# A recurrent and linear-attention decoder step: samples' output half a unit later, output sums 10 units behind the heads' opening, two tiles loaded with the others, heads' buffers 96 bytes on

## The chip, the cores and the metric

The kernel runs on one core of one Trainium2 chip. The time is that of the device for one execution, in microseconds, and what counts is the median over the runs of a kernel. The engines of the core each take their instructions in their own order: TensorE (PE in the profile, its weight loads PEld), VectorE (DVE), ScalarE (ACT), GpSimd (POOL) and SyncE (SP). The last two mostly issue transfers here, ScalarE some of them. An instruction that waits holds up all that stand behind it on its engine.

## What is computed

One layer for one prompt of 2048 tokens and for 8 samples of one token each, with a model width of 1024. Cut to what matters:

```
ada = silu(c) @ w_ada + b_ada;  shift, scale, gate = split(ada, 3)
hn  = rmsnorm(x, g_norm) * (1 + scale) + shift
xa, za, q, k, v, glr, zg = split(hn @ w_in)          # one projection, 5136 columns
# group 1: a convolution over 4 tokens, gates, and a linear recurrence over tokens
xc  = conv_b + sum(xp[:, j:j+T] * conv_w[j] for j in range(4))
a   = exp(8 * sigmoid(xc @ w_gate_a + b_a) * log_sigmoid(lambda))
h_t = a_t * h_(t-1) + sqrt(1 - a_t^2) * sigmoid(xc @ w_gate_x + b_x) * xc
y_lru = h * silu(za)
# group 2: 4 heads of gated linear attention (key width 128, value width 256)
S_t = exp(log_alpha_t) * S_(t-1) + k_t^T v_t;   o_t = q_t S_t
y_gla = rmsnorm(o) * g_gla_norm * silu(zg)
y = rmsnorm(x + gate * (concat(y_lru, y_gla) @ w_out), g_final)
```

The outputs are y for the prompt and the samples and the new states of both groups. Everything is float32.

## The kernel before

A float32 product is made of three matmuls on two parts of each operand: a rounded part (names in h: `hh`, `xh`, `vh`) and the rest (names in l: `hl`, `xl`, `vl`). So most matmuls come in threes, such as L661 to L663 for projections and L346 to L348 for the values of a head. For the larger products the kernel uses seven sub-products of half the size instead of eight, with sums of operands prepared ahead.

The prompt is worked off in two halves of 1024 tokens; the samples ride behind the second half. In each half the four heads come in the order 3, 0, 1, 2 (`gla_head`), each followed by tiles of the recurrence (`lru`). Between the halves lie the products of the second half that are made by seven (`sums`, `gates_seven`, `lru_seven`), with buffers of a pool `sp` of their own. Last comes the output product (L1846).

The second half's input comes in eight tiles of 128 tokens, two to a group. `hn_load` (L245) reads the two tiles of a group, on SyncE; `normalize` takes their squares on ScalarE (L165), a reciprocal root on VectorE in twelve small instructions (L147 to L153), and scales the tiles (L181); `modulate` turns them on TensorE (L197) into `hh` and `hl`. `next_hn` (L1428) is called in small pieces between the projections of the last recurrence tile of the first half and of what follows. Tiles 2 to 6 lie in three buffers `xst` of pool `sp`; tiles 0, 1 and 7 lie in a ring `xt`.

A queue of due times sets the order of most of the work in the heads. `after(units, fn)` (L701) puts a step off until the clock has gone on by so many units; `tick` (L705) moves the clock on, about one unit to a projection, and runs what is due. In the second half a head's samples are handled by `sample_state` (L1091), twice, for four samples each: GpSimd issues a load of the head's states (L1100), ScalarE and VectorE update them (L1104, L1105), and three units later `sample_out` (L1109) takes the output on TensorE (L1114), adds both fours (L1119), takes the mean square (L165 and twelve small instructions) and scales the output (L1124). Then it calls `done`, which puts the output in `os_`.

The head's own output is `gla_out` (L1156): TensorE turns the output of the prompt's tokens (L1162), for the last segment puts the samples' output behind them (L1164), and VectorE multiplies both with the gate (L1167). `finish` (L1213) calls it, and for the last segment looks every half unit whether `os_` is there. The fourth head's last steps are run by `flush_gla`, with no projections of a next head between them.

`out_weights` (L800) makes the sums of the output weights ("output sums") in 16 steps. A step loads two blocks of the weights (L829, GpSimd), four units later multiplies them by the gate (two L850 of 128x512), takes four differences (L850, 128x256), in half of the steps splits two of them into two parts (L854 on ScalarE, L855 on VectorE), and stores all (L857, L864, GpSimd) for the output product. It stops ahead of the second half's products and goes on in `close_sp` (L1476), which opens the heads' pools `gp` and `hp` for the second half:

```
        if outw["next"] < 16:
            outw["stop"] = False
            after(4, lambda: out_weights(outw["next"]))
```

On VectorE these sums stand in one order with the work of the heads: the eviction of a chunk's output (L1081), the scaling of a segment's output (L1089), the convolution (L1278) and the split of its result (L1303).

Of the kernel before, what the change touches and what calls it, by code (L numbers as in the profile page):

```python
# [8 lines left out]
F32 = mybir.dt.float32  # L9
# [5 lines left out]
P = 128  # L15
# [34 lines left out]
def dram(ap, off, pattern):  # L50
    return bass.AP(tensor=ap.tensor, offset=ap.offset + off, ap=pattern)
# [3 lines left out]
def hybrid_kernel(ctx, tc, i, o):  # L55
# [127 lines left out]
    def normalize(pool, xt, m=P, tag="f512"):  # L183

        times(xt, scales(pool, squares(pool, xt, m, tag), len(xt), m), m)
# [59 lines left out]
    def hn_load(g, now=True):  # L245

        xt = []
        for j in range(2):
            q = 2 * g + j
            if q in (0, 1, 7):  # L250
                x = xp.tile([P, TH + NS], F32, tag="xt", name="xt")[:, :D]
            else:
                n = q - 2
                x = xst[n // 2][:, n % 2]
            t0 = TH + q * P
            SP.dma_start(x, i["x_prompt"][0, t0:t0 + P])
            xt.append(x)
        if now:
            normalize(xp, xt)
        return xt  # L260
# [176 lines left out]
    with tc.tile_pool(name="ada", bufs=1, side="right") as ap:  # L437
# [79 lines left out]
        with in_order():  # L517
# [24 lines left out]
            for c in range(1, 4):  # L542
                k = (2 * c, 2 * c + 1)
# [100 lines left out]
    gp = gpx.enter_context(tc.tile_pool(name="gp", bufs=1, side="right", reuse_waits="tile"))  # L644
# [56 lines left out]
    def after(units, fn, gla=False, val=False):  # L701
        clock[1] += 1
        heapq.heappush(pend, (clock[0] + units, clock[1], fn, gla, val))
# [10 lines left out]
    def flush_gla():  # L714
        while any(e[3] for e in pend):
            e = min(e for e in pend if e[3])
            pend.remove(e)
            heapq.heapify(pend)
            e[2]()
# [28 lines left out]
    outw = {"stop": False, "next": None, "busy": False}  # L748
# [342 lines left out]
    def sample_state(h, smp, b0, st, done):  # L1091

        if b0 == 0:
            st[:] = [cp.tile([P, NS, 32], F32, tag="sc", name="qm"), gp.tile([P, DV], F32, tag="os", name="os")]
            V.memset(st[0], 0.0)
        qm = st[0]
        vb = xp.tile([P, 4, DV], F32, tag="xt", name="xt")
        G.dma_start(vb, dram(vsd, (h * NS + b0) * DV, [[0, P], [DV, 4], [1, DV]]))
        s0 = xp.tile([P, 4, DV], F32, tag="xt", name="xt")
        G.dma_start(s0, i["state_gla"][0, b0:b0 + 4, h].rearrange("b k v -> k b v"))  # L1100
        for n in range(4):
            b = b0 + n
            V.tensor_copy(qm[:, b, b:b + 1], smp[:, 0, b:b + 1])
            S.activation(s0[:, n], s0[:, n], AF.Copy, scale=smp[:, 2, b:b + 1])  # L1104
            V.scalar_tensor_tensor(s0[:, n], vb[:, n], smp[:, 1, b:b + 1], s0[:, n],  # L1105
                                   op0=OP.mult, op1=OP.add)
        after(3, lambda: sample_out(h, b0, st, s0, done), True)
# [62 lines left out]
    def gla_head(half, h, wv=None, ahead=None):  # L1170
# [13 lines left out]
        prep, zs, os_, state = {}, {}, [None], []  # L1184
# [32 lines left out]
            gla_out(half, h, s, prep[s, "run"][1], os_[0] if s == 2 else None, [zs[s, 0], zs[s, 1]])  # L1217

        def sample(smp, b0):
            sample_state(h, smp, b0, state, lambda: os_.__setitem__(0, state[1]))  # L1220

        pk = None
        if not wv:
# [194 lines left out]
    def lru(half, js, wx=None):  # L1418
        xa_load, xa_unit, za_load, za_unit = lru_units(half)
        for j in js:  # L1420
            t = xa_load(j, wx)
            for s in range(len(t.segs)):
                xa_unit(t, s)
            za_load(t)
            for s in range(len(t.segs)):
                za_unit(t, s)

    def next_hn(xt, g, k):  # L1428

        modulate(xt[g], g, (k, k + 2))  # L1430
        if (g, k) == (0, 6):
            xt.append(hn_load(3, False))
        if (g, k) == (1, 2):
            normalize(xp, xt[3])

    def lru_last_a(js):

        xa_load, xa_unit, za_load, za_unit = lru_units(0)
        xt = [hn_load(0)]
        lru(0, js[:-2])  # L1440
        outw["stop"] = True
        lru(0, js[-2:-1])
        t = xa_load(js[-1])
        za_load(t)
        flush_gla()
        while outw["busy"]:
            heapq.heappop(pend)[2]()
        open_sp()
        xt += [hn_load(1), hn_load(2)]
        for s in range(2):  # L1450
            xa_unit(t, s)
            za_unit(t, s)
            for g in range(2 * s, 2 * s + 2):
                for k in range(0, KT, 2):
                    drips.append(lambda g=g, k=k: next_hn(xt, g, k))
# [20 lines left out]
    def close_sp():  # L1476
        nonlocal gp, hp
        spx.close()
        gp = gpx.enter_context(tc.tile_pool(name="gp", bufs=1, side="right", reuse_waits="tile"))
        hp = hpx.enter_context(tc.tile_pool(name="hp", bufs=1, reuse_waits="tile"))  # L1480
        if outw["next"] < 16:
            outw["stop"] = False
            after(4, lambda: out_weights(outw["next"]))

    def a21():
        return [(hh, hl)[u][:, :4, 512:TH] for u in range(2)]
# [190 lines left out]
    flush_gla()  # L1677
    while outw["busy"]:
        heapq.heappop(pend)[2]()
    gpx.close()  # L1680
    hpx.close()

# [375 lines left out]
    smp = {}  # L2058
# [117 lines left out]
    for n in range(2, 16):  # L2176
        g = n - 1
# [17 lines left out]
    for q in range(8):  # L2195
        g, k = 2 + q // 2, q % 2
# [63 lines left out]
```

## Time and profile before

| | us |
|---|---|
| median of 3 runs | 1456.41 |
| the three runs | 1750.81, 1455.38, 1456.41 |
| the profiled execution | 1454.69 |
| its span (first to last instruction) | 1452.9 |
| TensorE busy in it | 1424.1 |
| VectorE busy in it | 1051.5 |
| ScalarE busy in it | 689.6 |
| GpSimd busy in it | 220.0 |

The profile is one execution. Its times count from the start of the span; an engine is busy while an instruction of its own runs, and what it only issues (a transfer) isn't counted. A row of the timeline gives the start, how long it took, the engine, the line of the kernel, the operation and its tiles, and in brackets how long the engine had been idle before it and what ended that. A view of waits adds these up by the instruction that waited and the one that released it. The second half's heads run from about 708 to 1077 us, and the output product starts at about 1128. The mean granted clock of TensorE was 0.998 of full speed.

### The profile page before, as it was taken

How to read it: one execution, taken by the hardware profiler on the slowest of the kernel's cores; microseconds unless marked ns; L12 is line 12 of the kernel's file. 1: busy time of each engine (PE TensorE's matmuls, PEld its weight loads, DVE VectorE, ACT ScalarE, POOL GpSimd, SP SyncE). 2: the span in 40 equal slices, each digit the busy share in tenths (PEclk: the TensorE clock that was granted, in tenths of full speed). 3: DMA queues.
4: the chain of work that ended last, by engine and by line, in shares of the span. 5: the costliest groups of instructions: out<-in, count | busy, mean ns of one | idle time of the engine just before them, and what ended most of it. 6: DMA issues, size and time to landing. Idle time of an engine off the chain costs nothing. (4 is left out here: it accounts for less than half of the span.)

```text
span 1452.9 us, 23584 instructions
## 1 busy us (share of the span) xinstructions
PE 1424.1 (98%) x8741; PEld 1250.8 (86%) x8741; DVE 1051.5 (72%) x2477; ACT 689.6 (47%) x1251; POOL 220.0 (15%) x364
## 2 busy tenths in 40 slices
PE   7999999999999999999999999999999999999998
PEld 5888989899898988778999999999998887788886
DVE  5757657776676688955468687586788986688886
ACT  4644544662545358524353454535557622144342
POOL 0200111212122113100212322323100000000000
PEclk9999999999999999999999999999999999999999
DMA  9755775764666455667846565656562767694453
GB/s 328 268 185 175 260 262 203 249 236 165 199 209 203 148 179 207 207 221 237 292 158 201 186 217 184 220 186 209 184 226 83 276 221 272 232 362 131 139 171 116
DMA packets 161752, 305.33 MB, mean 210 GB/s; under 512 B 12962, under 2 KB 91458, under 8 KB 159197
## 3 DMA queue, kind: packets, MB, share of 16 engines
q1 hardware_dynamic: 106837, 217.39, 43.6%
q0 software_dynamic: 22752, 70.44, 14.3%
q10 hardware_dynamic: 32048, 16.00, 3.7%
q8 instruction: 69, 1.13, 0.3%
q14 instruction: 46, 0.38, 0.1%
HBM read 188.51 MB, written 115.33 MB: 209 GB/s over the span
## 5 line engine op out<-in xcount | busy, mean ns | idle before, releaser
L661 PE MATMUL acc<-hh,w 128*128 128x512 f32 (+3 forms) x1112 | 386.1, 347 | 0.5 <-DVE xb L999 0.2
L662 PE MATMUL acc<-hl,w 128*128 128x512 f32 (+3 forms) x1112 | 375.6, 338 | 0.2 <-DVE hl L205 0.2
L663 PE MATMUL acc<-hh,w 128*128 128x512 f32 (+3 forms) x1112 | 375.1, 337 | 0.0
L662 PEld LDWEIGHTS acc<-hl,w 128*128 128x128 f32 x1112 | 209.3, 188 | 18.1 <-issue 1.2
L661 PEld LDWEIGHTS acc<-hh,w 128*128 128x128 f32 x1112 | 209.2, 188 | 18.1 <-ACT tx L1318 0.9
L663 PEld LDWEIGHTS acc<-hh,w 128*128 128x128 f32 x1112 | 209.1, 188 | 16.3
L1846 PE MATMUL acc<-w,a 128*128 128x512 f32 (+1 forms) x792 | 184.8, 386 | 0.0
L1846 PEld LDWEIGHTS acc<-w,a 128*128 128x128 f32 x792 | 146.8, 188 | 33.2 <-issue 3.4
L346 PE MATMUL acc<-w,hh 128*128 128x256 f32 (+1 forms) x508 | 144.7, 285 | 0.0
L348 PE MATMUL acc<-w,hl 128*128 128x256 f32 (+1 forms) x508 | 143.5, 282 | 0.2 <-DVE hl L228 0.2
L347 PE MATMUL acc<-w,hh 128*128 128x256 f32 (+1 forms) x508 | 143.4, 282 | 0.0
L1846 PE MATMUL tp<-w,a 128*128 128x512 f32 x564 | 136.0, 391 | 0.0
L1846 PEld LDWEIGHTS tp<-w,a 128*128 128x128 f32 x564 | 105.2, 188 | 26.8 <-issue 5.2
L346 PEld LDWEIGHTS acc<-w,hh 128*128 128x128 f32 x508 | 95.5, 188 | 1.3 <-ACT zs L1128 0.4
L348 PEld LDWEIGHTS acc<-w,hl 128*128 128x128 f32 x508 | 96.2, 189 | 0.4 <-DVE hl L228 0.4
L347 PEld LDWEIGHTS acc<-w,hh 128*128 128x128 f32 x508 | 96.0, 189 | 0.2
L1128 ACT ACTIVATE zs<-acc 128x512 f32<-128x512 f32 (+3 forms) x70 | 34.3, 490 | 107.0 <-PE acc L663 104.0
L1696 ACT CAST a<-s 128x512 fp32r<-128x512 f32 x61 | 36.5, 619 | 96.1 <-issue 36.6
L1278 DVE SCALAR_TENSOR_TENSOR cv<-xa,vecT,cv 128x512 f32<-128x512 f32 (+2 forms) x120 | 76.3, 638 | 7.2 <-ACT cv L1276 6.7
L1129 DVE SCALAR_TENSOR_TENSOR zs<-zs,acc 128x512 f32<-128x512 f32 (+3 forms) x70 | 38.4, 548 | 46.7 <-ACT zs L1128 46.7
L957 ACT CAST vh<-acc 128x256 fp32r<-128x256 f32 x56 | 20.5, 369 | 94.2 <-PE acc L348 81.8
L958 DVE TENSOR_TENSOR vl<-acc,vh 128x256 fp32r<-128x256 f32 x56 | 23.3, 420 | 51.1 <-ACT vh L957 51.1
(403 smaller groups left out, 2746.4 us busy)
## 6 DMA issues: line engine op xcount, KB each, us to landing
parts<-w SPq DMA_DIRECT2D x37, 1024.0 KB
w<-parts SPq DMA_DIRECT2D x28, 1024.0 KB
wr<-in_w_in_dram SPq DMA_DIRECT2D x38, 512.0 KB
a<-mixd SPq DMA_DIRECT2D x63, 256.0 KB
w<-wd SPq DMA_DIRECT2D x12, 1024.0 KB
w<-twd SPq DMA_DIRECT2D x20, 512.0 KB
mixd<-zs ACTq DMA_DIRECT2D x34, 256.0 KB
wada<-in_w_ada_dram SPq DMA_DIRECT2D x16, 512.0 KB
```

What stands on the lines that cost most here:

```text
L346: PE.matmul(ps, hh[:, kt, c], hi[:, kt % 4], start=kt == 0, stop=False)
L347: PE.matmul(ps, hh[:, kt, c], lo[:, kt % 4], start=False, stop=False)
L348: PE.matmul(ps, hl[:, kt, c], hi[:, kt % 4], start=False, stop=kt == KT - 1)
L661: PE.matmul(ps[:, :n], hi[:, kt], a, start=kt == 0, stop=False)
L662: PE.matmul(ps[:, :n], hi[:, kt], b, start=False, stop=False)
L663: PE.matmul(ps[:, :n], lo[:, kt], a, start=False, stop=kt == KT - 1)
L958: V.tensor_tensor(lo, ps[:, :DV], hi.bitcast(F32), op=OP.subtract)
L1128: S.activation(z, ps, AF.Tanh, scale=0.5)
L1129: V.scalar_tensor_tensor(z, z, 1.0, ps, op0=OP.add, op1=OP.mult)
L1278: V.scalar_tensor_tensor(cv[:, cq], xa[:, cq.start + k:cq.stop + k], cw[k], cv[:, cq], op0=OP.mult, op1=OP.add)
L1696: S.copy(t[:, 0, k], (low(t) if src is None else src)[:, k])
L1846: PE.matmul(ps, t[:, u, k], w[:, v, k, c], start=(q < 3 or ps is own) and (k, u, v) == (0, 0, 0), stop=(k, u) == (3, 1), skip_group_check= ...
```

## The change

Four places change. The samples' `done` no longer puts the output into `os_` at once but half a unit later. The output sums go on 10 units behind the opening of the heads' pools instead of 4. Tile 7 of the second half goes into the free place of the third `xst` buffer instead of the ring, its group (tiles 6 and 7) is loaded with groups 1 and 2, and it is normalized one piece earlier. A tile of 24 floats a partition is allocated in `gp` behind all others; nothing writes or reads it, and the heads' buffers of the second half, which are laid out from the pool's end, lie 96 bytes lower.

```
--- before.py
+++ after.py
@@ -247,7 +247,7 @@
         xt = []
         for j in range(2):
             q = 2 * g + j
-            if q in (0, 1, 7):
+            if q < 2:
                 x = xp.tile([P, TH + NS], F32, tag="xt", name="xt")[:, :D]
             else:
                 n = q - 2
@@ -1217,7 +1217,7 @@
             gla_out(half, h, s, prep[s, "run"][1], os_[0] if s == 2 else None, [zs[s, 0], zs[s, 1]])
 
         def sample(smp, b0):
-            sample_state(h, smp, b0, state, lambda: os_.__setitem__(0, state[1]))
+            sample_state(h, smp, b0, state, lambda: after(0.5, lambda: os_.__setitem__(0, state[1]), True))
 
         pk = None
         if not wv:
@@ -1428,9 +1428,7 @@
     def next_hn(xt, g, k):
 
         modulate(xt[g], g, (k, k + 2))
-        if (g, k) == (0, 6):
-            xt.append(hn_load(3, False))
-        if (g, k) == (1, 2):
+        if (g, k) == (1, 0):
             normalize(xp, xt[3])
 
     def lru_last_a(js):
@@ -1446,7 +1444,7 @@
         while outw["busy"]:
             heapq.heappop(pend)[2]()
         open_sp()
-        xt += [hn_load(1), hn_load(2)]
+        xt += [hn_load(1), hn_load(2), hn_load(3, False)]
         for s in range(2):
             xa_unit(t, s)
             za_unit(t, s)
@@ -1480,7 +1478,7 @@
         hp = hpx.enter_context(tc.tile_pool(name="hp", bufs=1, reuse_waits="tile"))
         if outw["next"] < 16:
             outw["stop"] = False
-            after(4, lambda: out_weights(outw["next"]))
+            after(10, lambda: out_weights(outw["next"]))
 
     def a21():
         return [(hh, hl)[u][:, :4, 512:TH] for u in range(2)]
@@ -1677,6 +1675,7 @@
     flush_gla()
     while outw["busy"]:
         heapq.heappop(pend)[2]()
+    gp.tile([P, 24], F32, name="pad")
     gpx.close()
     hpx.close()
```

The number of matmuls and of the other operations on tiles is the same. What moves is shown at three places, before and after, as the instructions stand on an engine, without times; "x2" is two of a kind one after the other.

On TensorE, the end of the second of the second half's heads (head 0), before. L346 to L348 are the values of the next head; `acc_9505` is one of their accumulators, and `os` the samples' output.

```order
L348 MATMUL acc_9464<-w_9454,hl_128 128x256
L1162 MATMUL tp_9491<-ident_72,on_9147 128x128 x2
L1162 MATMUL tp_9498<-ident_72,on_9147 128x128 x2
L346 MATMUL acc_9505<-w_9452,hh_127 128x256
L347 MATMUL acc_9505<-w_9452,hh_127 128x256
L348 MATMUL acc_9505<-w_9452,hl_128 128x256
L1164 MATMUL tp_9491<-sel4_91,os_9047 128x8
L1164 MATMUL tp_9498<-sel4_91,os_9047 128x8
```

The same place after; `acc_9473` is what was `acc_9505`.

```order
L346 MATMUL acc_9473<-w_9422,hh_127 128x256
L347 MATMUL acc_9473<-w_9422,hh_127 128x256
L348 MATMUL acc_9473<-w_9422,hl_128 128x256
L1162 MATMUL tp_9503<-ident_72,on_9129 128x128 x2
L1164 MATMUL tp_9503<-sel4_91,os_9015 128x8
L1162 MATMUL tp_9510<-ident_72,on_9129 128x128 x2
L1164 MATMUL tp_9510<-sel4_91,os_9015 128x8
L346 MATMUL acc_9517<-w_9420,hh_127 128x256
```

L1162 stood ahead of that accumulator's 24 matmuls and L1164 behind the first three of them. Both now stand behind all 24. In the third head it is the same; in the first, L1164 moves back by 9. In the fourth, L1164 keeps its place among the projections.

On VectorE, between the halves: the start of the reciprocal root for tiles 6 and 7 (`rs_x`, `rs_t`, `rs_y`). Rows with - are of before, rows with + of after.

```order
 L205 TENSOR_TENSOR hl<-fs_5824,hh 128x2x256
-L1278 SCALAR_TENSOR_TENSOR cv<-xa,vecT,cv 128x512 x2
+L1278 SCALAR_TENSOR_TENSOR cv<-xa,vecT,cv 128x512
+L147 TENSOR_SCALAR rs_x<-ss 128x2
+L1278 SCALAR_TENSOR_TENSOR cv<-xa,vecT,cv 128x512
+L148 TENSOR_SCALAR rs_t<-rs_x 128x2
+L1385 COPY xa<-xac 128x3
+L149 TENSOR_SCALAR rs_y<-rs_t 128x2
+L151 TENSOR_TENSOR rs_t<-rs_y 128x2
 L205 TENSOR_TENSOR hl<-fs_5824,hh 128x2x256
+L152 SCALAR_TENSOR_TENSOR rs_t<-rs_t,rs_x 128x2
```

L147, which stood behind both L205 of this place and the next, now stands between two L1278, and the other small ones of the chain between large ones; the two L181 at its end stay behind L1296.

On VectorE, in the last head: four L850 of 128x256 of the step of the output sums that now falls here (`r` and `t` are its tiles).

```order
 L1303 TENSOR_TENSOR xl<-cv,xh 128x384
+L850 TENSOR_TENSOR t<-r 128x256
 L147 TENSOR_SCALAR rs_x<-oss 128x3
+L1049 TENSOR_TENSOR aml<-am,amh 128x256
+L850 TENSOR_TENSOR r<-r 128x256
+L148 TENSOR_SCALAR rs_t<-rs_x 128x3
+L1052 TENSOR_TENSOR kTl<-tp,kTh 128x256
+L850 TENSOR_TENSOR t<-r 128x256
+L149 TENSOR_SCALAR rs_y<-rs_t 128x3
 L1056 TENSOR_SCALAR S_116<-S_116,f 128x256
-L148 TENSOR_SCALAR rs_t<-rs_x 128x3
-L1049 TENSOR_TENSOR aml<-am,amh 128x256
```

The two L850 of 128x512 of the same step stand 10 instructions ahead of this, and its two L855 stand behind the next L1303, ahead of an L1167. In the first head of the second half one step less is found: six L850 and two L855 are gone from between the chunks of its first two segments. On GpSimd the step's loads and stores move along, so that in the last head two L857 stand ahead of the load L1100 of the second four samples, and one L1210 (the load of a gate) now stands behind that load instead of ahead of it.

More of the change, by code (lines that the diff above doesn't have):

```diff
@@ L249, in hn_load @@
             q = 2 * g + j
-            if q in (0, 1, 7):
+            if q < 2:
                 x = xp.tile([P, TH + NS], F32, tag="xt", name="xt")[:, :D]
@@ L1219, in sample @@
         def sample(smp, b0):
-            sample_state(h, smp, b0, state, lambda: os_.__setitem__(0, state[1]))
+            sample_state(h, smp, b0, state, lambda: after(0.5, lambda: os_.__setitem__(0, state[1]), True))
         pk = None
@@ L1430, in next_hn @@
         modulate(xt[g], g, (k, k + 2))
-        if (g, k) == (0, 6):
-            xt.append(hn_load(3, False))
-        if (g, k) == (1, 2):
+        if (g, k) == (1, 0):
             normalize(xp, xt[3])
@@ L1448, in lru_last_a @@
         open_sp()
-        xt += [hn_load(1), hn_load(2)]
+        xt += [hn_load(1), hn_load(2), hn_load(3, False)]
         for s in range(2):
@@ L1482, in close_sp @@
             outw["stop"] = False
-            after(4, lambda: out_weights(outw["next"]))
+            after(10, lambda: out_weights(outw["next"]))
     def a21():
@@ L1679, in hybrid_kernel @@
         heapq.heappop(pend)[2]()
+    gp.tile([P, 24], F32, name="pad")
     gpx.close()
```

## Prediction

> **What bounds the kernel now.** I read the head of the page first, then the list of what TensorE (PE) waited for, then busy time by stretches of 25 us, and last the timelines at each wait that the change touches.
>
> ```profile
> span 1452.9 us, 23584 instructions
> PE 1424.1 (98%) x8741; PEld 1250.8 (86%) x8741; DVE 1051.5 (72%) x2477; ACT 689.6 (47%) x1251; POOL 220.0 (15%) x364
> ```
>
> TensorE is the bound: it is idle for 1452.9 - 1424.1 = 28.8 us in all. No edit adds or removes a matmul, so everything the change can win lies in those 28.8 us, and everything it can lose is a new TensorE wait. Each row of the next answer reads "engine, written tile and line, who released it: us in total, times, longest".
>
> ```profile
> PE tp L1164 <- DVE os L1124: 2.6, 4, 1.1
> PE po L1072 <- DVE on L1081: 1.5, 2, 1.0
> PE acc L1561 <- DVE so L1497: 1.5, 2, 1.2
> PE acc L1315 <- DVE zs L1129: 1.4, 1, 1.4
> PE acc L1315 <- ACT tx L1318: 0.9, 1, 0.9
> PE acc L1561 <- DVE ra L1497: 0.8, 1, 0.8
> ```
>
> All but one of these are waits for VectorE (DVE). The stretches show where that engine is nearly full; the columns are the stretch, then busy time (and instructions) of PE, PEld, DVE, ACT and POOL, the granted TensorE clock, the DMA share and GB/s.
>
> ```profile
> 600.00:625.00 25.00, 22.74 (x98) 17.70 (x97) 23.21 (x24) 11.28 (x15) 0.60 (x1) 1.00 0.77 259
> 1075.00:1100.00 25.00, 22.89 (x143) 21.59 (x143) 23.49 (x54) 18.17 (x34) 0.00 (x0) 1.00 0.60 212
> ```
>
> The 600 stretch lies right behind the place where the tiles are scaled; the 1075 stretch right behind the last head, into which the change puts more VectorE work.
>
> **The samples' output, half a unit later.** TensorE takes its instructions in order, so an early L1164 (the matmul that puts the samples' rows into the gating sum) holds up the projections behind it.
>
> ```profile
> 804.64 0.28 PE L348 MATMUL acc<-w,hl 128*128 128x256 f32 x1
> 804.75 0.28 PE L346 MATMUL acc<-w,hh 128*128 128x256 f32 x1
> 805.55 0.61 PE L1164 MATMUL tp<-sel,os 128*128 128x8 f32 x4 [0.53 <-DVE os L1124]
> 1076.38 0.61 PE L1164 MATMUL tp<-sel,os 128*128 128x8 f32 x4 [1.05 <-DVE os L1124]
> ```
>
> Two projections start 0.11 us apart (804.64 to 804.75), so L1164 could have started at 804.86; it started at 805.55, a loss of 0.69. By the list above there are four such waits of 2.6 us together; without the 0.53 and 1.05 shown, the other two are about 0.5 each. In the order of the changed kernel, L1162 and L1164 of the first three heads of the second half stand 9 to 24 projections further back, at 0.11 us each 1.0 to 2.6 us later, more than the 0.69 that is missing. Gain: 3 x 0.69 = 2.1 us. The cover is the projections that stand in between; if the output on VectorE is itself later by over 0.3 us (1.0 - 0.69), the first head's wait starts to come back.
>
> The fourth head has no projections left to put in between, and its L1164 keeps its place. Its wait hangs on a chain from a state load that GpSimd issues:
>
> ```profile
> 1063.59 4.42 DMA xt<-in_state_gla_dram
> 1068.09 1.71 ACT xt L1104 x4
> 1070.57 1.25 ACT xl L1323
> 1072.09 1.14 ACT tg L1325
> ```
>
> There one L1210 issue now stands behind the load instead of ahead of it (0.54 by the GpSimd timeline),
>
> ```profile
> 1062.30 0.54 POOL L1210 DMA_DIRECT2D zs<-zgd  x1 [15.15 <-DVE S L1078]
> ```
>
> but in between ScalarE's L1323 and L1325 (1.25 and 1.14) hold the sum of squares back as before. Bounds 0 to 1.05; I take the half of it, 0.5, because the load is at the head of the chain and the two activations only partly hide it.
>
> **The output sums, 10 units instead of 4.** One step of them moves out of the first head of the second half into the last. A step is two L850 of 128x512, four of 128x256 and, in half of the steps, two L855.
>
> ```profile
> L850 DVE TENSOR_TENSOR r<-r,g x32: 668/684/693, 328.0 to 1014.2; 128x512 f32<-128x512 f32 x32
> L850 DVE TENSOR_TENSOR t<-r x32: 410/417/426, 329.8 to 1023.2; 128x256 f32<-128x256 f32 x32
> ```
>
> An L855 takes 0.42 too (next rows). That is 2 x 0.68 + 6 x 0.42 = 3.9 us of VectorE time at most. In the first head it comes off a place where TensorE waits:
>
> ```profile
> 774.46 0.28 PE L661 MATMUL acc<-hh,w 128*128 128x264 f32 x1
> 775.74 0.38 PE L1072 MATMUL po<-vh,amh 128*128 128x256 f32 x1 [1.00 <-DVE on L1081]
> 774.07 0.42 DVE L855 TENSOR_TENSOR p<-r,p 128x256 fp32r<-128x256 f32 x1
> 774.41 0.42 DVE L855 TENSOR_TENSOR p<-t,p 128x256 fp32r<-128x256 f32 x1
> 774.74 0.61 DVE L1167 SCALAR_TENSOR_TENSOR zs<-tp,gsc,zs 128x384 f32<-128x384 f32 x1
> 775.27 0.41 DVE L1081 COPY on<-po 128x256 f32<-128x256 f32 x1
> ```
>
> L1072 would have followed at 774.46 + 0.12; it came 1.16 later, when L1081 had emptied its bank. Ahead of L1081 stood two L855, 0.34 and 0.33 from start to start, and before them the step's six L850. With all of these gone L1081 is over 1.16 earlier: gain 1.2 (0.67, the two L855 alone, to 1.16).
>
> In the last head the step goes in among these:
>
> ```profile
> 1048.80 0.62 DVE L1278 SCALAR_TENSOR_TENSOR cv<-xa,vecT,cv 128x384 f32<-128x384 f32 x1 [2.30 <-ACT cv L1276]
> 1057.35 0.43 DVE L1303 TENSOR_TENSOR xl<-cv,xh 128x264 fp32r<-128x264 f32 x1
> 1059.12 0.62 DVE L1167 SCALAR_TENSOR_TENSOR zs<-tp,gsc,zs 128x384 f32<-128x384 f32 x1 [1.35 <-PE tp L1162]
> 1058.60 0.81 PE L1162 MATMUL tp<-ident,on 128*128 128x128 f32 x6
> ```
>
> The two large L850 fit into the idle 2.30 at 1048.80, and the two L855 into the 1.35 at 1059.12. The four small L850 have no gap: at 0.34 from start to start they push all behind them by 1.35. The last L1089, whose output L1162 turns, ended at 1057.43 (rows follow each other 0.08 before an end: 774.07 + 0.42 against 774.41, and L1303 starts at 1057.35). It would end at 1058.78, L1162 could start 0.06 behind that (L1081 ends at 775.68, L1072 starts at 775.74), and it started at 1058.60: 0.24 late, and a TensorE wait costs 0.16 more than its gap (0.69 against 0.53 above). Queued behind it are all later projections. Cost 0.4; 0 if the gaps take the push up, 1.35 if the two large L850 don't fit their gap either. The step's two ScalarE casts and its GpSimd stores stand beside work that nobody waits for, except the load of the fourth head's chain, which is a rival below.
>
> **The last two tiles, sooner.** The fourth pair's last tile is now read with the other five:
>
> ```profile
> 577.02 0.16 DVE L147 TENSOR_SCALAR rs_x<-ss 128x2 f32<-128x2 f32 x1
> 577.22 0.17 DVE L148 TENSOR_SCALAR rs_t<-rs_x 128x2 int32<-128x2 int32 x1
> 582.10 1.10 DVE L181 TENSOR_SCALAR xst<-xst,rs 128x1024 f32<-128x1024 f32 x1
> 583.12 0.73 DVE L181 TENSOR_SCALAR xt<-xt,rs 128x1024 f32<-128x1024 f32 x1
> 583.35 0.30 PE L197 MATMUL tp<-ident,xst 128*128 128x128 f32 x1 [1.22 <-DVE xst L181]
> 583.91 0.33 PE L197 MATMUL tp<-ident,xt 128*128 128x128 f32 x1 [0.26 <-DVE xt L181]
> ```
>
> On SyncE one L256 moves ahead of one weight load, which is issued only when TensorE has freed a buffer, long behind it: nothing. Its landing is earlier than before, and the room that it lands in isn't used by others: nothing. The chain from L147 to the two L181 takes 5.1 us (577.02 to 582.10). Its twelve tiny instructions depend on each other and start 0.2 apart (577.02 to 577.22); where nothing large stands between two, VectorE has that 0.2 for one of them. In the new order nearly each has a large instruction beside it that had to be done anyway. Eight of them that no longer stand bare are 8 x 0.2 = 1.6 us, an estimate from these rows. TensorE waited 1.22 + 0.26 = 1.48. Gain 1.3, a little under both (0 if the tiny ones cost as much between large ones as alone; 1.5 if both waits go).
>
> The first of these L181 took 1.10, the second 0.73 for the same tile size; the first lay beside a GpSimd L204:
>
> ```profile
> 580.03 1.15 POOL L204 TENSOR_SCALAR hh<-fs 128x512 fp32r<-128x512 f32 x1 [0.60 <-ACT fs L201]
> 581.90 0.75 POOL L204 TENSOR_SCALAR hh<-fs 128x512 fp32r<-128x512 f32 x1 [0.72 <-POOL hh L204]
> ```
>
> So the neighbour costs an L181 0.37, and the earlier pair could meet both L204: one more 0.37 at most, and a sum of 4.3 instead of the 4.7 below. [...]
>
> **Heads' buffers 96 bytes on.** A 128x24 tile is allocated, never written. No instruction is added. The same L850 on different buffers took 668 to 693 ns and 410 to 426: no sign that a place in memory matters. Cost 0, at most the width of that spread, 0.03 us an instruction, on an engine that isn't the bound.
>
> **Sum.** 2.1 + 0.5 + 1.2 - 0.4 + 1.3 = 4.7 us off the profiled execution, which took 1454.69 (span 1452.9 and 1.8 around it): 1450.0. The other runs shown took 1455.38 and 1456.41 (and one 1750.81, far off); the lower is 0.7 above the profiled one. I add that and forecast 1451. By the bounds of the terms it lies between 1449.5 (2.1 + 1.05 + 1.2 + 1.5 = 5.9 off) and 1454 (2.1 + 0 + 0.7 - 1.35 + 0 = 1.4 off).
>
> **Rivals.** *Given back.* VectorE is busy 23.21 of 25 us in the 600 stretch, where L1561 waits 1.5 + 0.8 for it; if VectorE itself and not TensorE sets the pace there, the 1.3 comes back as a longer wait, and likewise the later L1167 of the three heads push L1331 and what follows, so that 2.1 returns. Left: 0.5 + 1.2 - 0.4 = 1.3; 1454.69 - 1.3 + 0.7 = 1454. For it: nearly all waits are for VectorE. Against it: in the heads VectorE has gaps such as the 2.30 and 1.35 above.
>
> *GpSimd beside the tiles' scaling.* If both L181 wait for a whole L204 (1.15 and 0.75, less the 0.37 paid already), 1.5 us are lost and the gain of 1.3 is gone: 1452. Against it: an L181 beside an L204 took 0.37 longer, not a whole L204.
>
> *The last head's state load, slower than before.* GpSimd issues in order, and the last two stores of the moved step, which wait for L855, now stand just ahead of the load at 1063.59.
>
> ```profile
> DMA to landing us min/median/max: 4.2/5.9/8.8
> ```
>
> The load landed in 4.42 then, near the least of its eight; at the longest it is 8.8, 4.4 more. With the push of 1.35 and two L855 of 0.33 ahead, less the 0.54 of L1210, it lands 5.9 later. Everything from L1104 to L1164 follows one for one, and TensorE has nothing else queued. Against the 2.1 + 1.2 + 1.3 = 4.6 won elsewhere that is 1.3 slower: 1454.69 + 1.3 + 0.7 = 1457. It decides from a load that lands 4.6 us later. Against it: with L855 at 1059.12 and two issues of some 0.54 behind, the stores are out by 1061, and GpSimd then waits for L1078 as it did before, until 1062.30.
>
> *More.* If the waits of 0.9 and 1.4 at L1315 (about 1095 and 1114) shrink as well because VectorE starts sooner into the full stretch, 2.3 more go: 1448.
>
> **Chances.** The sum 0.52, given back 0.20, GpSimd beside the scaling 0.08, the late load 0.12, more 0.06, a loss over 2% that no view shows 0.02. What a measurement tells from no change is about 2%, 29 us; all of TensorE's idle time is 28.8, so faster by that is next to impossible (0.01, from the "more" case), and same is 0.97. Range 1447.5 to 1457: from the "more" case to the late load.
>
> **What would show it.** Right: no TensorE wait on os at L1164 in the first three heads; no L1072 wait in the first head's last chunk; the L197 waits on L181 under 0.3 together. Wrong: the wait at the fourth L1164 over 1.05, or L1561 waiting over 2.3, or a new wait at L1162 over 1.

## The result and the profile after

| | before | after |
|---|---|---|
| median of 22 runs, us | 1455.97 | 1453.41 |
| ratio, 95% interval | | 0.9984 [0.9977, 0.9991] |
| profiled execution, us | 1454.69 | 1452.05 |
| its span, us | 1452.9 | 1450.3 |

The change makes the kernel 2.3 us faster, between 1.3 and 3.3. (One run of each kernel, 1750.81 and 3627.53 us, was disturbed and isn't in the ratio.) The head of the page after:

```profile
span 1450.3 us, 23579 instructions
PE 1425.6 (98%) x8741; PEld 1253.1 (86%) x8741; DVE 1051.2 (72%) x2477; ACT 690.0 (48%) x1251; POOL 220.5 (15%) x364
```

TensorE's idle time fell from 28.8 to 24.7 us, by 4.1, and still the span is only 2.6 shorter: TensorE is busy 1.5 us longer with the same 8741 matmuls. That part lies ahead of everything that was changed: up to L1162 of the first half, at 225 us, TensorE is idle 1.6 us less and busy 1.8 us more, and no time is won. Behind that place its idle time fell by 2.6 and the time by 2.8. What it waits for, after, in the rows that bear on the change (engine, written tile and line, releaser: us in total, times, longest):

```profile
PE po L1114 <- DVE xt L1105: 2.1, 1, 2.1
PE acc L1559 <- DVE so L1495: 1.4, 2, 1.2
PE acc L1315 <- DVE zs L1129: 1.4, 1, 1.4
PE acc L1315 <- ACT tx L1318: 1.1, 1, 1.1
PE tp L1164 <- DVE os L1124: 0.8, 1, 0.8
PE acc L1559 <- DVE ra L1495: 0.8, 1, 0.8
PE acc L661 <- DVE zs L1129: 0.7, 1, 0.7
```

Three of the four waits at L1164 are gone, and those at L1072 and L197. New are 2.1 us at L1114 and 0.7 at L661. (L1495 and L1559 are L1497 and L1561 of before.) Where on the way the time went shows when the same matmul starts in both traces:

| matmul | before | after | difference | since the row above |
|---|---|---|---|---|
| L1162, first half | 225.59 | 225.81 | +0.22 | |
| L1561/L1559, behind the tiles | 614.57 | 613.75 | -0.82 | tiles -1.0 |
| L1072, first head | 775.74 | 773.44 | -2.30 | 10 units -1.5 |
| L1072, first head, next chunk | 794.43 | 791.43 | -3.00 | wait there -0.7 |
| L663, second head | 882.30 | 878.75 | -3.55 | first L1164 -0.6, all else 0.0 |
| L1114, second head | 888.56 | 887.34 | -1.22 | new wait +2.3 |
| L346, second head | 890.64 | 890.93 | +0.29 | lower clock +1.5 |
| L1042, third head | 925.49 | 924.40 | -1.09 | second L1164 -0.7, L1042 -0.7 |
| L661, fourth head | 1011.02 | 1008.13 | -2.90 | third L1164 -0.7, others -1.1 |
| L1164, fourth head | 1076.38 | 1073.51 | -2.87 | 0.0 |
| L1315, behind the heads | 1113.86 | 1111.19 | -2.67 | +0.2 |

The second head gives back 3.8 us: the difference goes from -3.55 to +0.29. The timeline of TensorE there, after:

```profile
884.94 0.28 PE L663 MATMUL acc<-hh,w 128*128 128x264 f32 x1
887.34 0.89 PE L1114 MATMUL po<-xt,qm 128*32 128x256 f32 x8 [2.12 <-DVE xt L1105]
888.55 0.42 PE L1316 MATMUL acc<-xl,wg 128*128 128x264 f32 x1
888.77 0.42 PE L1317 MATMUL acc<-xh,wg 128*128 128x264 f32 x1
```

and busy time and granted clock in short stretches (the columns are those of the prediction; the clock is the third from the right):

```profile
884.00:887.00 3.00, 1.22 (x11) 1.01 (x9) 1.44 (x4) 1.71 (x4) 0.00 (x0) 1.00 0.23 31
887.00:889.00 2.00, 1.66 (x12) 1.02 (x13) 0.94 (x3) 0.00 (x0) 0.77 (x1) 0.65 0.84 328
889.00:891.00 2.00, 2.00 (x11) 2.00 (x11) 1.26 (x2) 1.74 (x5) 0.00 (x0) 0.50 0.99 405
891.00:893.00 2.00, 2.00 (x19) 2.00 (x19) 1.63 (x11) 1.97 (x2) 0.00 (x0) 1.00 0.53 153
```

Matmuls of 264 columns start 0.22 apart (888.55 to 888.77) and take 0.42; before the wait they took 0.28. So the wait costs its 2.3 and then 1.5 more at a clock of 0.50. L1114 is the second output of the second head's samples. It waits for L1105, that for ScalarE's L1104, and that for the state load L1100, which GpSimd can issue only when the first output of this head, also at L1114, has freed the load's buffer. Both outputs and L1104, before:

```profile
880.38 0.64 PE L1114 MATMUL po<-xt,qm 128*32 128x256 f32 x8
885.92 1.71 ACT L1104 ACTIVATE xt<-xt,smp 128x256 f32<-128x256 f32 x4 [0.68 <-DMA xt<-in_state_gla_dram]
888.56 0.64 PE L1114 MATMUL po<-xt,qm 128*32 128x256 f32 x8
```

and after:

```profile
878.18 0.64 PE L1114 MATMUL po<-xt,qm 128*32 128x256 f32 x8
885.01 1.71 ACT L1104 ACTIVATE xt<-xt,smp 128x256 f32<-128x256 f32 x4 [2.06 <-DMA xt<-in_state_gla_dram]
```

GpSimd after:

```profile
875.32 1.44 POOL L829 DMA_DIRECT2D r<-in_w_out_dram  x2 [4.34 <-DMA wd<-r]
876.75 0.55 POOL L1210 DMA_DIRECT2D zs<-zgd  x1
878.74 0.55 POOL L1210 DMA_DIRECT2D zs<-zgd  x1 [1.45 <-DVE rs_t L148]
879.28 0.55 POOL L1204 DMA_DIRECT2D out_dram<-S  x1
879.94 0.76 POOL L1100 DMA_DIRECT2D xt<-in_state_gla_dram  x1
```

and before:

```profile
880.59 0.56 POOL L1204 DMA_DIRECT2D out_dram<-S  x1 [7.40 <-DVE S L1078]
881.50 0.76 POOL L1100 DMA_DIRECT2D xt<-in_state_gla_dram  x1 [0.35 <-issue]
882.25 0.54 POOL L1210 DMA_DIRECT2D zs<-zgd  x1
```

TensorE comes to this place 3.55 us sooner, the load is issued only 1.56 sooner (881.50 to 879.94). The first output itself is only 2.20 sooner, as it now stands seven matmuls further back in TensorE's order: 43 matmuls lie between the two outputs instead of 50, and without waits TensorE needs 7.04 us from one to the other instead of 8.18. Then the load is issued 1.12 us behind the end of the first output instead of 0.48, for a second gate load (L1210) now stands ahead of it; the loads of r (L829) are out before the buffer is free. And from issue to L1104 it takes 5.07 us instead of 4.42. So the chain got 1.3 us longer and TensorE's way to its end 1.1 us shorter, where 0.4 us had been to spare.

### The profile page after: what moved, and what is told of

Read it like the earlier page. It is cut to its first block, busy times and chain, and to the rows that moved or that the text cites. A ratio compares the mean times of both kernels' runs of the same rounds, so it can differ in the third digit from the quotient of the medians.

```text
span 1450.3 us, 23579 instructions
## 1 busy us (share of the span) xinstructions
PE 1425.6 (98%) x8741; PEld 1253.1 (86%) x8741; DVE 1051.2 (72%) x2477; ACT 690.0 (48%) x1251; POOL 220.5 (15%) x364
## 5 line engine op out<-in xcount | busy, mean ns | idle before, releaser
L661 PE MATMUL acc<-hh,w 128*128 128x512 f32 (+3 forms) x1112 | 386.2, 347 | 1.3 <-DVE zs L1129 0.7
L663 PE MATMUL acc<-hh,w 128*128 128x512 f32 (+3 forms) x1112 | 375.6, 338 | 0.0
L661 PEld LDWEIGHTS acc<-hh,w 128*128 128x128 f32 x1112 | 209.3, 188 | 20.0 <-ACT tx L1318 0.9
L663 PEld LDWEIGHTS acc<-hh,w 128*128 128x128 f32 x1112 | 209.1, 188 | 16.8 <-issue 0.4
L346 PE MATMUL acc<-w,hh 128*128 128x256 f32 (+1 forms) x508 | 144.9, 285 | 0.1
L348 PE MATMUL acc<-w,hl 128*128 128x256 f32 (+1 forms) x508 | 143.6, 283 | 0.0
L346 PEld LDWEIGHTS acc<-w,hh 128*128 128x128 f32 x508 | 96.8, 191 | 1.3 <-ACT zs L1128 0.4
L348 PEld LDWEIGHTS acc<-w,hl 128*128 128x128 f32 x508 | 96.4, 190 | 0.0
L1278 DVE SCALAR_TENSOR_TENSOR cv<-xa,vecT,cv 128x512 f32<-128x512 f32 (+2 forms) x120 | 77.1, 645 | 6.0 <-ACT cv L1276 5.7
L1129 DVE SCALAR_TENSOR_TENSOR zs<-zs,acc 128x512 f32<-128x512 f32 (+3 forms) x70 | 38.6, 551 | 47.3 <-ACT zs L1128 47.2
```

The lines of the kernel that those rows point to most:

```text
L346: PE.matmul(ps, hh[:, kt, c], hi[:, kt % 4], start=kt == 0, stop=False)
L348: PE.matmul(ps, hl[:, kt, c], hi[:, kt % 4], start=False, stop=kt == KT - 1)
L661: PE.matmul(ps[:, :n], hi[:, kt], a, start=kt == 0, stop=False)
L663: PE.matmul(ps[:, :n], lo[:, kt], a, start=False, stop=kt == KT - 1)
L1129: V.scalar_tensor_tensor(z, z, 1.0, ps, op0=OP.add, op1=OP.mult)
L1278: V.scalar_tensor_tensor(cv[:, cq], xa[:, cq.start + k:cq.stop + k], cw[k], cv[:, cq], op0=OP.mult, op1=OP.add)
```

## The experiments

None of the twelve leaves anything out. Ratios are to the kernel before on the same chip.

| run | what differs | median, us | ratio, 95% interval |
|---|---|---|---|
| e1 | before + half unit | 1456.43 | 0.9998 [0.9990, 1.0007] |
| e2 | before + 10 units | 1456.82 | 0.9994 [0.9984, 1.0003] |
| e3 | before + tiles | 1454.44 | 0.9985 [0.9974, 0.9996] |
| e4 | changed - 96 bytes | 1452.91 | 0.9973 [0.9964, 0.9982] |
| e5 | before + load of the tile alone | 1455.74 | one run (before 1456.43) |
| e6 | changed, second output half a unit later | 1459.26 | 1.0012 [1.0000, 1.0024] |
| e7 | changed, second output a unit later | 1456.23 | 1.0000 [0.9991, 1.0009] |
| e8 | changed, 4 units | 1455.75 | 0.9997 [0.9987, 1.0007] |
| e9 | changed, once more | 1454.12 | 0.9981 [0.9972, 0.9990] |
| e10 | changed, L1204 issued by ScalarE | 1453.84 | 0.9979 [0.9971, 0.9987] |
| e11 | e10, two L1210 issued by ScalarE | 1453.86 | 0.9984 [0.9975, 0.9992] |
| e12 | changed, first output two units sooner | 1457.95 | 1.0009 [0.9998, 1.0019] |

### The half unit alone (e1)

```
-            sample_state(h, smp, b0, state, lambda: os_.__setitem__(0, state[1]))
+            sample_state(h, smp, b0, state, lambda: after(0.5, lambda: os_.__setitem__(0, state[1]), True))
```

> The kernel before with the half unit alone. Theory (each wait at L1164 in the first three heads is worth 0.65 to 0.69 us, and the load of the second head's state has 0.3 us to spare): three waits gone, 2.0 us less, at most 0.4 given back at L1114 of the second head: 1.6 to 2.0 us faster. Rival (the waits return elsewhere, as VectorE has the same work to do): within 0.5 us of before, with a new TensorE wait for VectorE between 806 and 830 us. The other parts' waits (L1072 at 775 and 794, L197 at 583) stay as they are in both.

The three waits at L1164 went as expected, and there is no wait at L1114, but no time is won. The rival has the time right and the place wrong, for a new wait of 4.7 us stands in the third head. TensorE:

```profile
927.42 0.80 PE L1042 MATMUL tp<-xb,e 128*128 128x128 f32 x2 [4.67 <-DVE xb L1027]
```

VectorE:

```profile
917.02 1.30 DVE L850 TENSOR_TENSOR r<-r,g 128x512 f32<-128x512 f32 x2 [4.00 <-DMA r<-in_w_out_dram]
...
926.82 0.55 DVE L1027 SCALAR_TENSOR_TENSOR xb<-acc,xb 128x384 f32<-128x384 f32 x1
```

GpSimd:

```profile
904.62 0.54 POOL L1210 DMA_DIRECT2D zs<-zgd  x1 [14.34 <-DVE zs L1129]
...
909.48 1.43 POOL L829 DMA_DIRECT2D r<-in_w_out_dram  x2 [0.87 <-DMA wd<-r]
```

and GpSimd in the kernel before:

```profile
898.82 0.54 POOL L1210 DMA_DIRECT2D zs<-zgd  x1 [7.80 <-DVE tx L1332]
...
906.65 1.44 POOL L829 DMA_DIRECT2D r<-in_w_out_dram  x2 [1.55 <-DMA wd<-r]
```

The outputs are turned later, so the gates' buffers come free later. The next head's gate load L1210 waits 14.34 us on GpSimd instead of 7.80, and the loads of r behind it are issued at 909.48 instead of 906.65, while TensorE is ahead. VectorE's L850 waits 4.00 us for r; L1027 is queued behind it, and TensorE waits for L1027. Behind the wait the clock is down again, to 0.50:

```profile
928.00:930.00 2.00, 2.00 (x11) 2.00 (x10) 1.18 (x2) 1.97 (x3) 1.47 (x3) 0.50 0.64 143
```

### The 10 units alone (e2)

```
-            after(4, lambda: out_weights(outw["next"]))
+            after(10, lambda: out_weights(outw["next"]))
```

> The kernel before with the 10 units alone. Theory (the moved step frees VectorE in the first head; the second head's state load is queued on GpSimd behind one more gate load and TensorE runs into it): the waits at L1072 near 775 and 794 gone, some 2.3 us less; a wait at L1114 of the second head near 888 of 0.5 to 1.5 us, short of the one in the whole change since TensorE comes there 1.5 us later without the other parts; in sum 0.5 to 2 us faster. Rival (the 10 units alone make the late load, whatever the other parts do): a wait of 2 us or more there with a clock below 1.00 behind it, and no gain or a loss.

```profile
889.55 0.64 PE L1114 MATMUL po<-xt,qm 128*32 128x256 f32 x8 [2.10 <-issue]
```

The rival's wait, 2.10 us, with the rest of the change left out: the 10 units alone make the load late. The seven matmuls are moved here too (43 between the two outputs), and in none of the runs with 4 units (50 in e1, e3, e5 and e8); why the 10 units move them wasn't followed up. The clock stayed at 1.00 behind it in this profile. The gains in the first head were there (L1072 at 774.50 instead of 775.74, and no wait at the next chunk), and the wait took them: 0.9994.

### The 4 units with all the rest (e8)

```
-            after(10, lambda: out_weights(outw["next"]))
+            after(4, lambda: out_weights(outw["next"]))
```

> The changed kernel with 4 units again instead of 10 (half unit, tiles and 96 bytes stay). Theory (the half unit holds the gates' buffers longer, the next head's gate load L1210 then waits some 14 us on GpSimd instead of 8, the loads of r behind it come 3 us late, VectorE's L850 and, behind it, L1027 wait, and TensorE at L1042; the 10 units move these loads off that place): the wait of some 4.7 at L1042 near 925 is back, with a clock below 1.00 behind it, no wait over 1 at L1114 near 888; the tiles' 1.7 are kept: 0.998 to 0.9995 of before. Rival (the wait in the half unit alone was one run's late transfer): no such wait, 0.9955 to 0.9975 of before.

```profile
PE tp L1042 <- DVE xb L1027: 3.3, 2, 2.3
...
PE acc L661 <- DVE xb L1009: 1.8, 1, 1.8
PE acc L661 <- DMA w<-parts: 1.6, 1, 1.6
```

The wait at L1042 is back, with 2.35 instead of 4.67 us and at 928.5, and the wait at L1114 near 888 is 0.28. With it the change's gain is gone: 0.9997, just above the theory's range. The theory holds in the place, not in the size of that wait; 1.8 and 1.6 us of waits at L661 ahead of it come on top. Here too GpSimd's L1210 waits long, 13.88 us. So the 10 units take away what the half unit costs. The reverse doesn't hold: the wait at L1114 is 2.10 us in e2 and 2.12 in the changed kernel. The 10 units with the tiles and without the half unit were not run.

### The two tiles (e3), and the load alone (e5)

e3 is the kernel before with the tile's part of the diff; e5 differs from e3 in

```
-        if (g, k) == (1, 0):
+        if (g, k) == (1, 2):
```

> The kernel before with the two tiles alone. Theory (the waits at L197 go, 2.0 us with their refill, and a new wait of 0.66 at L661 near 577 for L1129, pushed back by the root's small instructions, takes 1.05): 0.9 us faster, and carried on to the end, as the second head's state load follows TensorE. Rival (the gain is lost where TensorE next waits for something that does not move): 0 to 0.3 faster, with a longer wait at L1497's readers near 615 to 621 or at L1114 near 888.

> The kernel before with tile 7 loaded with the others, but normalized at its old place (behind the second small piece of group 1 after this one). Theory (the gain of the tiles comes from where the root's small instructions stand on VectorE, not from the load): the waits at L197 near 583 stay at 1.2 and 0.3, no new wait at L661 near 577, time as before within the scatter of single runs (2 us). Rival (the earlier load itself is what the scaling waited for): the L197 waits gone here too.

In e3 the waits at L197 are gone, and L661 waits 0.93 for L1129 near 578. From the trace the place is worth 0.7 us (the matmul behind it stands at +0.09 ahead and -0.61 behind, against before); 0.2 more are gone by 614 us, and 0.7 more at the second L1072 of the first head, which nothing in the edit touches. That wait hangs on the first head's state load: ScalarE waits 3.61 us for it before and 3.54 in e1, but 2.76 to 2.86 in e2, e3, e5, e8 and the changed kernel, and only the first two have the wait. So the 10 units are not needed to take it away; why the load lands sooner isn't shown. The timed runs, 0.9985, agree with the sum and not with the rival's 0 to 0.3.

In e5 the waits at L197 are gone too, and L661 waits 1.10: the place where the normalizing is called isn't what counts, and that theory fell. But the load alone also moves VectorE's order (two L205 stand between the root's small instructions, one in the kernel before), so whether the earlier landing or the order took the waits away stays open. The new wait stands at the same place in both and in the changed kernel, here VectorE and TensorE of that:

```profile
577.24 0.69 DVE L1129 SCALAR_TENSOR_TENSOR zs<-zs,acc 128x512 f32<-128x512 f32 x1
...
581.18 1.78 DVE L181 TENSOR_SCALAR xst<-xst,rs 128x1024 f32<-128x1024 f32 x2
```

```profile
577.98 0.39 PE L661 MATMUL acc<-hh,w 128*128 128x256 f32 x1 [0.66 <-DVE zs L1129]
```

The two L181 come 0.9 sooner (581.18 instead of 582.10), but the eviction L1129 now ends behind half of the chain, and TensorE needs its bank first.

### Without the 96 bytes (e4), and the changed kernel again (e9)

e4 leaves out the line

```
-    gp.tile([P, 24], F32, name="pad")
```

> The changed kernel without the 96 bytes. Theory (where the heads' buffers lie costs nothing): the time of the changed kernel, within 0.5 us, and the same waits at the same places, L1114 of the second head among them. Rival (the place in memory decides about some of the transfers or the VectorE times): over 1 us from the changed kernel, and other instruction durations in the heads.

> The changed kernel once more, beside the next two. Theory: the wait at L1114 in the second head (near 888) is there again with 1.9 to 2.2 us, since GpSimd's order sets it and not chance; behind it the clock may or may not fall (it did in two of three profiles with such a wait). Time 0.9975 to 0.9990 of before. Rival (the wait was one profile's late transfer): under 1 us there.

e4 has the waits of the changed kernel (1.97 at L1114 near 888). Its 0.9973 lies below the changed kernel's 0.9984 and 0.9981, with overlapping intervals, and e9 ran on another chip: no gain of the 96 bytes is seen; whether they cost something under 1.5 us isn't settled. e9 has 2.21 us at L1114, with the clock at 0.50 behind it: the wait is no accident of one profile.

### The second output later (e6, e7)

```
-        after(3, lambda: sample_out(h, b0, st, s0, done), True)
+        after(3.5 if b0 and h != HEADS[3] else 3, lambda: sample_out(h, b0, st, s0, done), True)
```

(e7 has 4 in place of 3.5.)

> The changed kernel with the second output of a head's samples (L1114 and what follows) half a unit later in the first three heads. Theory (the state load of the second head lands 2 us after TensorE wants it; VectorE, GpSimd and the transfer have no other part in it): L1114 there stands some 28 matmuls, 3.3 us, later, its wait of 2.1 is gone, and the lower clock behind it too; 2 to 3.8 us below the changed kernel, 0.9955 to 0.997 of before. Rival (L1114 is only the first to wait for a late GpSimd queue): a wait of about 2 us at another TensorE line within 30 us behind it, and the time of the changed kernel.

> As the one before, with a whole unit instead of half. Theory (half a unit is enough, more makes the gates' buffers come free later, so that GpSimd's gate loads and the weight loads queued behind them are late, as in the half unit alone, where VectorE waited 4.00 us for r): not better than half a unit, and slower by up to 6 us if a wait at L1042 of 2 us or more turns up in one of the heads. Rival (the later the output, the fewer waits): as fast as half a unit or faster.

The wait at L1114 near 888 is gone in both, and e6's rival was right about the other lines; the time is worse than it said, 1.0012:

```profile
PE tp L1164 <- DVE os L1124: 5.8, 4, 2.0
PE acc L661 <- DVE S L1056: 2.0, 1, 2.0
```

is e6. The output that is taken later reaches L1164 later. That line waits 1.66, 1.95 and 1.25 us in the first three heads, and 2.0 us at L661 follow. The state load, its update, the output and L1164 are one chain; a later step in the middle only moves the wait to its end. e7 is no better than the kernel before either. The wait at L1042 that its theory feared isn't there, and it is not slower than e6, as its rival had it; its longest wait is 2.78 us, at the second L1164.

### The state load sooner (e10, e11, e12)

e10 takes the store of the final state off GpSimd's queue, e11 two gate loads besides, e12 frees the load's buffer sooner:

```
-                G.dma_start(o[4][0, 0, h], St[h])
+                S.dma_start(o[4][0, 0, h], St[h])
```

```
-                G.dma_start(z[:, :n], zgd[2 * h + dt][:, c0:c0 + n])
+                (S if s == 2 else G).dma_start(z[:, :n], zgd[2 * h + dt][:, c0:c0 + n])
```

```
-        after(3, lambda: sample_out(h, b0, st, s0, done), True)
+        after(3 if b0 else 1, lambda: sample_out(h, b0, st, s0, done), True)
```

> The changed kernel with the store of a head's final state (L1204) issued by ScalarE instead of GpSimd, TensorE's order unchanged. Theory (the second head's wait follows the issue of the state load L1100, which stands behind L1204 on GpSimd): L1100 is issued 0.5 to 0.7 us sooner, the wait at L1114 in the second head is shorter by as much (1.3 to 1.6), and the wait at the fourth L1164 shrinks too (0.8 to 0.2 or 0.5); 0.5 to 1.3 us below the changed kernel, up to 3 where the clock holds. Rival (the wait follows the landing, which is the transfers' own): the load lands at the same time however early it is issued, and both waits stay.

> As the one before, and the two gate loads of a head's last segment (L1210, 128x264) issued by ScalarE too, so that nothing stands ahead of the second state load on GpSimd but its own other load and the wait for its buffer, which the first L1114 frees. Theory: L1100 issued about 1.1 us sooner than in the changed kernel, the wait at L1114 in the second head 0.9 to 1.2; in the fourth head's chain another 0.5 or so; 1 to 2 us below the changed kernel, up to 3.5 with the clock. Rival (ScalarE, which takes its instructions in order, waits at L1210 for a gate buffer as GpSimd did, with L165 and L1318 behind it): new TensorE waits at L1315 or for ScalarE, no gain.

> The changed kernel with the first output of a head's samples (the first L1114, which frees the buffer that the second state load L1100 waits for) one unit after its states are ready instead of three; the second output keeps its place in TensorE's order. Theory (the second load is late because GpSimd can issue it only when the first L1114 has freed its buffer, and then stands behind other issues): L1100 of the second head is issued 4 us or more sooner, ahead of the loads of r and of L1204, and the wait of some 2.1 at the second L1114 near 888 is gone with the lower clock behind it; in the fourth head the load is sooner as well and the waits at L1114 and L1164 there (0.5 and 0.9) shrink; 2.5 to 5 us below the changed kernel, 0.9945 to 0.9965 of before. Rival (as in the half unit later: TensorE finds another late step in the same heads): a new wait of 1 to 2 us at L1072, L1042 or L661 there, since r is now loaded behind the states, and the time of the changed kernel, 0.9975 to 0.9985.

The load's buffer is freed by the first L1114. GpSimd in e11:

```profile
879.60 0.75 POOL L1100 DMA_DIRECT2D xt<-in_state_gla_dram  x1 [2.01 <-PE po L1114]
```

From the end of the first L1114 to the issue of L1100 it is 1.12 us in the changed kernel, 0.96 in e9, 0.88 in e10 and 0.35 in e11, and the wait at the second L1114 is 2.12, 2.21, 1.93 and 1.39. From issue to L1104 the four take 5.07, 5.32, 5.12 and 5.11 us. Both stretches together are 6.19, 6.28, 6.00 and 5.46, each time 4.07 more than the wait: the wait follows issue and landing one for one. GpSimd's queue is worth 0.7 us of it; 1.39 are left in e11 though the load is issued 0.35 us behind the first output, sooner than before (0.48), so the rest is the seven matmuls and the landing. The clock holds at 1.00 behind e11's. e10 fell short of its theory, with the issue 0.24 sooner instead of 0.5 or more, and in both the wait at the fourth L1164 rose to 1.07 instead of shrinking. Neither is faster than the changed kernel (0.9984, 0.9981): in e11 TensorE waits 0.86 at L661 near 918 for VectorE, which it did not in the changed kernel, and the fourth head's two waits, at L1114 and L1164, are

```profile
PE tp L1164 <- DVE os L1124: 1.1, 1, 1.1
...
PE po L1114 <- PE acc L663: 0.8, 1, 0.8
```

instead of 0.1 and 0.8 in the changed kernel's profile and 0.5 and 0.9 in e9's. The theory was right about a part of the wait and wrong about what it is worth.

In e12 the first output stands earlier in TensorE's order, the load is issued at 874.17, 5.8 us sooner, and the second L1114 doesn't wait in any head. Other waits come, as the rival said, mostly at other lines than it named:

```profile
PE tp L1164 <- DVE stT L1339: 2.6, 1, 2.6
PE tp L1162 <- DVE on L1089: 2.0, 3, 1.1
PE pkv L1068 <- ACT kTh L1051: 1.8, 1, 1.8
```

and the kernel is slower than the changed one, as slow as before. No version beats the changed one beyond its interval.

## Why the prediction was right, and where it was off

The time, 1453.41, lies in the range, the direction was right, and the gain of 2.3 us is half of the 4.7 of the sum. All three signs of being right came, and none of the signs of being wrong: what took half of the gain lies at a line that no sign watched. Term by term, from the table of starting times:

- The half unit, 2.1: 0.6 + 0.7 + 0.7 = 2.0 in the changed kernel. Right in place and size. What it holds up wasn't asked: the gates' buffers. e1 shows that price, 4.67 us of wait and the clock of 0.50 behind it, which the changed kernel doesn't pay only because the 10 units move r.
- The fourth head, 0.5: the wait went from 1.05 to 0.83, so 0.2.
- The 10 units in the first head, 1.2: the wait at L1072 near 775 is gone as worked out, 1.5 with what comes ahead of it. The one at 794, which the sum left where it was, is gone as well, for 0.7 more; the tiles alone do that too (e3), so it isn't the 10 units' own.
- The 10 units in the last head, a cost of 0.4: 0.2 or less.
- The tiles, 1.3: the two waits of 1.48 are gone, but the new wait of 0.66 at L661 is the neighbour of that gain: about 1.0 in the changed kernel, 0.7 in e3. The small instructions that were to lie beside large ones lie ahead of an eviction for which TensorE waits.
- GpSimd beside the tiles' scaling: the two L181 took 1.78 together, against 1.75 from the start of the first to the end of the second before. The rival's whole L204 was not paid, neither trace shows an L181 that waits for one, and the row's 0.37 stayed as it was.
- The 96 bytes, 0: nothing shown to the contrary.
- L1042, no term: the list of waits in the prediction left its row out (1.5 us in all), and its wait of 0.56 in the third head is gone, for 0.7. Another 1.1 is won behind it that isn't L1164.

The step that failed is that the 10 units were taken to matter in the first and the last head alone, with stores that "stand beside work that nobody waits for, except the load of the fourth head's chain". A late state load is what happened, but in the second head and not in the fourth, and only in part as the rival had it. Moving the start of the output sums shifts all that comes later, TensorE's order too: the first output of the second head, which frees the load's buffer, stands seven matmuls further back (1.1 us), one more gate load stands ahead of the load on GpSimd (0.6), and the load takes 0.65 us longer to land. e2 shows it with the 10 units alone. Whether the landing is slower because of the change isn't shown: e8, with 4 units, has the same 5.07.

The price is 2.3 us of wait and 1.5 at the clock of 0.50. The places where time was won add up to 7.0 in the table; these 3.8 and 0.5 in small amounts go off, which leaves the 2.6 between the two traces. What the sum didn't have (0.7 at 794, 0.7 at L1042, 1.1 behind it) covers 2.5 of the 3.8. That the time came out as near as it did is luck to that extent.

The two edits in the heads don't add: 0.9998 and 0.9994 alone, and with the tiles kept, 0.9997 for the half unit without the 10 units. The tiles alone, 0.9985, are within the interval of the whole. In time, then, the whole change is hardly more than the tiles alone, and that the two others together give anything above them isn't shown.

## What to carry to other kernels

When a step of a background stream is moved, list where each of its later steps lands on the in-order queues, and what urgent load then stands behind which wait; the first and the last place are not enough. Compare TensorE's order in all heads as well: an instruction that frees a buffer counts for the load behind it, however little it costs itself (the first L1114 takes 0.64 us). A wait that is taken away moves TensorE forward, and the next thing that it meets is whatever doesn't move forward with it: here loads issued by GpSimd and tied to a buffer's release, 1.56 us sooner where TensorE came 3.55 sooner. And an instruction that is put off keeps its inputs' buffers: ask who waits for those (in e1 L1210, for 14.34 us instead of 7.80).

## What was not expected of the hardware

In the profiles before and after, waits of TensorE of 1.2 to 1.4 us behind the first 40 us of the span left the granted clock at 1.00 (before, 1.22 at L197 near 583, 1.20 at L1561 near 617 and 1.39 at L1315 near 1114; after, 1.21 at L1559 near 617 and 1.37 at L1315 near 1111). Of the 15 waits in the heads of 1.58 us and more in all profiles, 12 were followed by a clock of 0.50, with 1.66 us the shortest of these (e6, at L1164 near 811); the other three (2.10 in e2, 1.83 and 1.58 in e8) were not. In the changed kernel that costs 1.5 us on top of the wait.

The granted clock in short stretches shows more of it. Each stretch at 0.50 that ends before the span does lasts 3.4 us or twice that (887.59 to 891.01 in the changed kernel, 925.00 to 931.80 in e1), and within one profile the stretches start whole multiples of 3.413 us apart: in e6 at 812.96, 905.12 and 925.60, which is 27.0 and 6.0 times, and in the changed kernel at 24.02 and 887.59, which is 253.0 times. So in these two profiles the clock fell only at moments of one beat, wherever the wait lay. All 12 waits in the heads that brought the lower clock had 1.66 us or more between two such moments. The 1.58 us of e8 did not bring it, nor did its 1.83, which a moment cuts into 1.23 and 0.60; e2's profile has no lower clock that would show the beat. In the first 30 us, where short waits follow each other, 1.37 us of idle time between two moments were enough once (before, 8.85 to 12.27) and 1.53 were not (before, 22.51 to 25.92), so idle time alone doesn't decide it.
